# Attention's output products taken two tiles at a time, a rotary table repeated through DRAM, and a parity mask spread by loads

## The chip, the cores and the metric

The kernel runs on one core of one Trainium2 chip. Its time is in microseconds (us) of the device for one whole execution, from launch to the last store. All engines of the core run beside each other, each through its own list of instructions in order: PE (matrix products), ACT (copies and functions), DVE (elementwise work), POOL (elementwise work and masks), and SP (it only issues DMA transfers). An instruction begins when everything it waits for on other engines has been signalled. Products accumulate in PSUM banks; everything else stands in SBUF, 128 partitions wide.

## What the kernel computes

One decoder block over 1024 positions and 1024 channels: a norm, one wide input projection, two mixers that work from it, a merge, and a gated convolutional MLP. The parts that the change touches are those of the attention mixer:

```python
proj = h @ w_in[layer]
z_a, q, k, v, gate_logits = jnp.split(proj, splits, axis=-1)
q = apply_partial_rope(q.reshape(b, s, N_ATTN_HEADS, HEAD_DIM), cos, sin)
k = apply_partial_rope(k.reshape(b, s, N_ATTN_HEADS, HEAD_DIM), cos, sin)
# three groups of 4 heads: (window, dilation) = (128,1), (512,4), (2048,16)
for g, (window, dil) in enumerate(DILATED_GROUPS):
    o, lse = banded_window_attention(residue(q), residue(k), residue(v), window // dil)
alpha = softmax(lses over the groups)
y_b = einsum('bshg,bshgd->bshd', alpha, o_all)          # groups mixed by their denominators
```

Rotary turning covers the first quarter of each head's 64 channels (`t1*cos - t2*sin`, `t1*sin + t2*cos`). In group 1 a position's residue is its number modulo 4; in group 2 modulo 16, where the kernel puts two residues into one tile of 128 positions and a parity mask keeps them apart.

## The kernel before

**Products.** The large matrix products are taken in float32 as three products of split parts. Each weight block is split into a high part (`hi`, an ACT copy, L313) and a remainder (`lo`, a DVE subtraction, L314). The input projection goes by pairs of column blocks, numbered n (from 3 or 4 on in what follows; 5 and 6 are the ones looked at). For each pair PE makes seven products in the order P1, P6, P2, P7, P5, P4, P3, each 12 matmuls of 128x512 (L545). Their split weights stand in a ring of four slots in `G1` (`OPS_IN = 4`): the split for one product can be written only when the product four places earlier is done. Before P6 of a pair come three DVE sums of weight blocks (L278, L279, L280); L278 makes the block that P7 uses (`wt`, one buffer), L280 the one that P6 uses. Before P4 comes L283.

**Results.** P1 is copied out of its bank by ACT (L573); P2 then accumulates into the same bank as P1, after that copy; P2 is copied out by ACT (L577). P6, P7, P5, P4 and P3 are added to the copied values by DVE (L575, L580, L582, L585, L588). There are three such banks. P7's bank is the one that P4 uses two products later, and P5's is the one that P3 uses.

**Side work.** Everything that isn't an input product is hung between them by due times: `after(lag, fn)` runs `fn` so many half products (6 matmuls) later. Pairs 0 to 2 are the gating mixer's, then come three pairs of each attention group (q and k with their rotary part, the rest of q and k, v), groups in the order 1, 2, 0, and then the rest. In each group eight tiles T of 128 queries follow each other, every five half products: load, turn (scale), scores (`sc`), transposes of the probabilities (`pp`), and the product with v (`pu`, L935, 8 or 16 small matmuls), whose result ACT copies with stride 4 (group 1) or 8 (group 2) into a tile `o` of the whole group (L942), or without a stride into `YC` (group 0). After the last tile `o` is stored to DRAM.

**Rotary table.** Angles and sines are made by DVE, POOL and ACT in [position, (block, frequency)] form, spread over heads by 16 ACT copies, transposed by 4 x 4 PE transposes (`rot`, L2537), and copied into `YC` by ACT (L2538). `rope` (L794 to L796) applies it: six DVE operations for a pair, whose operand from `YC` is read with stride 4 in group 1, 8 in group 2 and 1 in group 0, and then four stores (L798).

**Parity mask.** One small matmul of a sign vector by itself (`pg`, L1099), a DVE operation, a POOL selection.

**Mix.** After the three groups, `mix_groups` loads for each half of the positions, each channel half and each group the weights `wb` and (groups 1 and 2) the outputs `ob`, multiplies them on DVE (L1057) and adds them to `YC` (L1060).

**Order.** PE's order is as written throughout. ACT's and DVE's are as written until product 18 of the input projection; behind it, and for SP's DMA issues everywhere, the framework's scheduler sets them when the kernel is built.

Of the kernel before, what the change touches and what calls it, by code (L numbers as in the profile page):

```python
# [20 lines left out]
P = 128  # L21
# [73 lines left out]
def block_kernel(  # L95
# [711 lines left out]
    def by_channel(t):  # L807
        return t.rearrange("(c p) s -> p c s", p=P)
# [7 lines left out]
    class Attend:  # L816
# [5 lines left out]

        def __init__(self, g, T, vts, out):
            self.g, self.T, self.vts, self.out = g, T, vts, out
# [86 lines left out]
        def turn_p(self):  # L911
            pT = at.tile([P, NH * 2, P], F32, name=f"pT_{self.name}", tag="pT", bufs=1)
# [14 lines left out]
        def product(self):  # L927
            pu = ps_x.tile([P, 2, P], F32, name=f"pu_{self.name}", tag="pu")
            n = len(self.parts)
            for pair in range(2):  # L930
                for k, s in enumerate(self.parts):
                    vt = self.vts[self.halves[s]]
                    for h in (2 * pair, 2 * pair + 1):
                        r = h % 2 * HD
                        nc.tensor.matmul(  # L935
                            pu[r : r + HD, pair, :],
                            vt[:, h * HD : (h + 1) * HD],
                            self.pT[:, h * n + k, :],
                            start=k == 0,
                            stop=k == n - 1,  # L940
                        )
# [4 lines left out]
        def columns(self):  # L946

            T = self.T
            if self.g == 0:
                return self.out[:, :, T * P : (T + 1) * P]  # L950
            if self.g == 1:
                r, bb = T // 2, T % 2
                return self.out[:, :, bb * HALF + r : (bb + 1) * HALF : 4]
            return self.out[:, :, T::8]

        def start(self, s):
            after(max(1, s - 4), self.load)
            after(s, self.turn)
            after(s + 3, self.score)
            after(s + 8, self.turn_p)  # L960
            after(s + 13, self.product)

    def attention(g, ct):
# [14 lines left out]
        out = at.tile([P, 2, S], F32, name=f"o_{g}", tag="o", bufs=1) if g else YC  # L978
        for T in range(8):
            Attend(g, T, vts, out).start(4 + 5 * T)  # L980
# [54 lines left out]
    def mix_groups(pool):  # L1035
# [5 lines left out]
        def load(h, c, g):  # L1041
# [8 lines left out]
            if g:  # L1050
                o = pool.tile([P, HALF], F32, name=f"ob_{h}_{c}_{g}", tag="ob", bufs=4)
                nc.sync.dma_start(o, by_channel(summed_d[g])[:, c, hs])
            got[h, c, g] = wb, o

        def mix(h, c, g):
            wb, o = got[h, c, g]
            tt(o, o, wb, ALU.mult)  # L1057
            if g:
                y = YC[:, c, h * HALF : (h + 1) * HALF]
# [12 lines left out]
    def open_attention():  # L1072
# [8 lines left out]
        sign = at.tile([P, 2, 256], F32, name="sign", tag="vt", bufs=4)[0:1, 0, 0:P]  # L1081
        nc.gpsimd.memset(mask, 0.0)
        nc.gpsimd.memset(sign[:, 0::2], 1.0)
        nc.gpsimd.memset(sign[:, 1::2], -1.0)
# [19 lines left out]
        after(8, parity_mask)  # L1104

# [77 lines left out]
    rot_halves = []  # L1183

    def rot_bank(name):
        if not rot_halves:
            t = ps_x.tile([P, 2, HALF], F32, name=name, tag="sc")
            rot_halves.extend((t[:, 1], t[:, 0]))
        return rot_halves.pop()
# [1405 lines left out]
```

## Time and profile before

| | us |
|---|---|
| median of 3 runs | 1343.32 (1343.31 to 1344.57) |
| the profiled execution, whole | 1342.83 |
| its span, first to last instruction | 1341.0 |
| what lies around the span | 1.83 |
| PE busy in the span | 1332.4 (99%) |
| DVE busy | 1037.5 (77%) |
| ACT busy | 648.4 (48%) |
| POOL busy | 283.9 (21%) |

The granted TensorE clock was 0.999 on the mean. The busy share of an engine says how much of the span it had an instruction running; only the engine on the chain that ended last sets the time directly. A matmul's record is some 0.39 us long for 128x512, but the next one begins 0.227 us after it (12 matmuls in 2.72 us), so stretches on PE are read from one start to the next.

### The profile page before, as it was taken

What the parts mean: (1) busy time and instruction counts of PE and PEld (TensorE: products, weight loads), DVE (VectorE), ACT (ScalarE), POOL (GpSimd) and SP (SyncE); (2) the same over time, 40 slices, a digit from 0 to 9 for tenths busy, and PEclk for the clock granted to TensorE, in tenths of its full rate; (3) what the DMA queues carried; (4) which work ended last, traced back from release to release, by engine and by line L of the source; (5) the groups of instructions that cost most, each with busy time, mean ns of one, the idle gap of its engine ahead of it and who ended that gap; (6) DMA issues with size and microseconds to landing.
All of it is one profiled execution on the core that took longest, in us unless ns stands there. A gap on an engine that the chain in (4) does not pass through costs nothing.

```text
span 1341.0 us, 19015 instructions
## 1 busy us (share of the span) xinstructions
PE 1332.4 (99%) x6405; PEld 1100.5 (82%) x6405; DVE 1037.5 (77%) x1808; ACT 648.4 (48%) x1267; POOL 283.9 (21%) x270
## 2 busy tenths in 40 slices
PE   9999999999999999999999999999999999999997
PEld 8888888888888888888888888888888888888886
DVE  7989696886768957759789789777777778576675
ACT  7762566666633325245365333433343335454453
POOL 1121000000000000120010337656565653000002
PEclk9999999999999999999999999999999999999999
DMA  9436444545439733975650324444445538986663
GB/s 353 108 98 186 118 139 132 159 148 168 130 107 273 272 108 121 300 254 189 198 178 17 126 97 154 166 165 165 163 151 173 175 123 293 396 313 222 197 205 126
DMA packets 148305, 240.19 MB, mean 179 GB/s; under 512 B 18320, under 2 KB 58864, under 8 KB 148208
## 3 DMA queue, kind: packets, MB, share of 16 engines
q1 hardware_dynamic: 145968, 234.99, 53.6%
q0 software_dynamic: 1088, 2.10, 0.9%
q10 hardware_dynamic: 1152, 1.89, 0.4%
q8 instruction: 51, 0.84, 0.3%
q14 instruction: 46, 0.38, 0.1%
HBM read 170.91 MB, written 64.34 MB: 175 GB/s over the span
## 4 chain that ended last, share of the span: by engine, by line
PE 98%; DVE 1%; ACT 0%; issue 0%; POOL 0%; POOLq 0%; DVEq 0%; ACTq 0%
PE in_P L545 30%; PE uP L2016 21%; PE dn L2298 15%; PE up L2016 9%; PE wo_P L1847 5%; PE pa L1477 5%; PE pl L618 3%; PE pu L1996 2%; PE pb L1477 2%; PE pu L935 1%; PE pp L916 1%; PE pm L733 1%; PE sc L865 1%; PE ht L1751 1%; PE sc L869 0%; PE avt L971 0%
## 5 line engine op out<-in xcount | busy, mean ns | idle before, releaser
L545 PE MATMUL in_P<-R,G 128*128 128x512 f32 x1008 | 237.3, 391 | 0.0
L545 PEld LDWEIGHTS in_P<-R,G 128*128 128x128 f32 x1008 | 187.4, 188 | 38.8 <-issue 0.3
L2298 PE MATMUL dn<-R 128*128 128x512 f32 x924 | 209.6, 389 | 0.0
L2298 PEld LDWEIGHTS dn<-R 128*128 128x128 f32 x924 | 173.4, 188 | 36.0
L170 ACT ACTIVATE R<-up 128x512 fp32r<-128x512 f32 x109 | 65.8, 623 | 122.9 <-DVE up L280 105.6
L2016 PE MATMUL uP<-G,R 128*128 128x512 f32 x504 | 121.4, 389 | 0.0
L2016 PE MATMUL uP<-R 128*128 128x512 f32 x504 | 121.1, 389 | 0.0
L313 ACT ACTIVATE G<-wr 128x512 fp32r<-128x512 f32 x126 | 78.4, 628 | 88.1 <-PE in_P L545 61.2
L2016 PE MATMUL up<-G,R 128*128 128x512 f32 x504 | 120.3, 389 | 0.0
L545 PE MATMUL in_P<-G,G 128*128 128x512 f32 x504 | 119.9, 391 | 0.0
L314 DVE TENSOR_TENSOR G<-wr,G 128x512 fp32r<-128x512 f32 x126 | 86.7, 689 | 42.7 <-ACT G L313 41.8
L2016 PEld LDWEIGHTS uP<-G,R 128*128 128x128 f32 x504 | 94.4, 188 | 20.2 <-issue 0.4
L2016 PEld LDWEIGHTS up<-G,R 128*128 128x128 f32 x504 | 94.6, 188 | 19.7
L2016 PEld LDWEIGHTS uP<-R 128*128 128x128 f32 x504 | 94.6, 188 | 19.6
L545 PEld LDWEIGHTS in_P<-G,G 128*128 128x128 f32 x504 | 93.7, 188 | 19.6 <-issue 0.3
L171 POOL TENSOR_TENSOR G<-wbs,G 128x512 fp32r<-128x512 f32 x12 | 17.0, 1432 | 437.9 <-ACT G L170 437.9
L171 POOL TENSOR_TENSOR R<-up,R 128x512 fp32r<-128x512 f32 x55 | 79.4, 1456 | 13.4 <-ACT R L170 12.1
L170 ACT ACTIVATE R<-db 128x512 fp32r<-128x512 f32 x77 | 48.0, 625 | 53.4 <-PE dn L2298 43.8
L171 DVE TENSOR_TENSOR R<-db,R 128x512 fp32r<-128x512 f32 x77 | 53.6, 700 | 24.9 <-ACT R L170 24.8
L1477 PE MATMUL pa<-R,G 128*128 128x512 f32 x288 | 67.9, 389 | 0.0
L1477 PEld LDWEIGHTS pa<-R,G 128*128 128x128 f32 x288 | 54.1, 188 | 11.2
L545 PE MATMUL in_P<-G 128*128 128x512 f32 x252 | 61.5, 391 | 0.0
(303 smaller groups left out, 2355.3 us busy)
## 6 DMA issues: line engine op xcount, KB each, us to landing
up<-in_w_up_dram SPq DMA_DIRECT2D x44, 512.0 KB, 4.1
wr<-in_w_in_dram SPq DMA_DIRECT2D x42, 512.0 KB, 4.1
dA<-gd SPq DMA_DIRECT2D x55, 256.0 KB, 4.7
dS<-gS SPq DMA_DIRECT2D x44, 256.0 KB, 4.5
db<-wT SPq DMA_DIRECT2D x44, 256.0 KB, 4.5
gd<-Y SPq DMA_DIRECT2D x42, 256.0 KB, 2.0
db<-in_w_down_dram SPq DMA_DIRECT2D x33, 256.0 KB, 4.9
gated<-C SPq DMA_DIRECT2D x32, 256.0 KB, 2.4
```

Of the source, the lines that this page charges most:

```text
L170: nc.scalar.activation(hi, src, AF.Copy)
L171: fn = lambda: lo_eng.tensor_tensor(lo, src, f32(hi), ALU.subtract)
L313: lambda: nc.scalar.activation(op[:, 0], src, AF.Copy),
L314: lambda: nc.vector.tensor_tensor(op[:, 1], src, f32(op[:, 0]), ALU.subtract),
L545: nc.tensor.matmul(acc, op[:, w, kt, :], left[LEFT[name], kt][:, a, :], start=opened and i == 0, stop=i == len(HIGH_FIRST) - 1, skip_group ...
L618: nc.tensor.matmul(lead_banks[b][:, cs], raw_x[h, kt][:, a, c * P : (c + 1) * P], lead_op(kt, w, cs), start=kt == 0 and p == 0 and cs.star ...
L733: nc.tensor.matmul(acc[hs], v[:, hs], wspT[:, (c * 2 + s) // 3, :], start=True, stop=True)
L1477: nc.tensor.matmul(acc, unit[a][kt // 4][:, kt % 4, :], two(R, 8 * h + kt)[:, b, :], start=n == 0 and i == 0, stop=n == len(kts) - 1 and i ...
L1847: nc.tensor.matmul(acc, left[LEFT[name], kt][:, a, blk * P : (blk + 1) * P], out_ops[s][:, w, :], start=name not in SHARED and kt == 0 and ...
L1996: nc.tensor.matmul(acc, plain_up[which, k][:, w, kt, :], left[f"A{h + 1}{k + 1}", kt][:, a, :], start=n == 0 and i == 0, stop=n == KT - 1 ...
L2016: nc.tensor.matmul(acc, op[w][:, kt, :], left[LEFT[name], kt][:, a, :], start=opened and i == 0, stop=i == len(HIGH_FIRST) - 1, skip_group ...
L2298: nc.tensor.matmul(accs[blk], dops[s][:, 0, a, blk * P : (blk + 1) * P], dops[s][:, 1, w, :], start=SEQ[j] not in CONTINUES and kt == 0 an ...
```

## The change

Four edits in one diff.

1. *Two tiles per output product.* An even tile T only keeps its transposed probabilities (two buffers of `pT`); the odd tile makes the products of both into one bank and copies 128x512 at once. In groups 1 and 2 the copy is contiguous, into a small tile `o` that is stored to DRAM for each pair of tiles.
2. *Mix.* `ob` is therefore loaded in residue order, and `wb` and the piece of `YC` are read (and `YC` written) through views with stride 4 (group 1) or 8 (group 2). In group 2 `ob` comes by two loads.
3. *Rotary table.* One PE transpose of the sines, two ACT copies, three stores to DRAM, eight DMAs inside DRAM that repeat the rows over heads, and one load into `YC`.
4. *Parity mask.* POOL writes two rows with alternating entries; they go to DRAM and come back by two loads, each spread over 64 partitions. `causal` follows at a due time of its own.

```diff
-    summed_d = {g: dram.tile([256, S], F32, name=f"od{g}") for g in (1, 2)}
+    summed_d = {g: dram.tile([4, P, 2, 2, P], F32, name=f"od{g}") for g in (1, 2)}
+    stripe_d = dram.tile([1, 2, P], F32, name="stripe")
...
-            pT = at.tile([P, NH * 2, P], F32, name=f"pT_{self.name}", tag="pT", bufs=1)
+            pT = at.tile([P, NH * 2, P], F32, name=f"pT_{self.name}", tag="pT", bufs=2)
...
         def product(self):
-            pu = ps_x.tile([P, 2, P], F32, name=f"pu_{self.name}", tag="pu")
...
-            nc.scalar.activation(self.columns(), pu, AF.Copy)
-            if self.T == NB - 1 and self.g:
-                nc.sync.dma_start(by_channel(summed_d[self.g]), self.out)
+            pu = ps_x.tile([P, 2, 2, P], F32, name=f"pu_{self.name}", tag="pu")
+            for t, one in enumerate((self.before, self)):
+                n = len(one.parts)
+                for pair in range(2):
+                    for k, s in enumerate(one.parts):
+                        vt = one.vts[one.halves[s]]
+                        for h in (2 * pair, 2 * pair + 1):
+                            r = h % 2 * HD
+                            nc.tensor.matmul(
+                                pu[r : r + HD, t, pair, :],
...
+            T0 = self.T - 1
+            if self.g == 0:
+                dst = YC[:, :, T0 * P : (T0 + 2) * P].rearrange("p c (t q) -> p t c q", t=2)
+                nc.scalar.activation(dst, pu, AF.Copy)
+            else:
+                o = at.tile([P, 2, 2, P], F32, name=f"o_{self.name}", tag="o", bufs=2)
+                nc.scalar.activation(o, pu, AF.Copy)
+                nc.sync.dma_start(summed_d[self.g][T0 // 2], o)
...
-            after(s + 13, self.product)
+            if self.before:
+                after(s + 13, self.product)
...
-                nc.sync.dma_start(o, by_channel(summed_d[g])[:, c, hs])
-            got[h, c, g] = wb, o
+                src = summed_d[g]
+                if g == 1:
+                    nc.sync.dma_start(
+                        o.rearrange("p (r q) -> p r q", r=4), src[:, :, h, c, :].rearrange("r p q -> p r q")
+                    )
+                else:
+                    js = slice(h * HD, (h + 1) * HD)
+                    for t in range(2):
+                        nc.sync.dma_start(
+                            o.rearrange("p (r t q) -> p t r q", r=4, t=2)[:, t],
+                            src[:, :, t, c, js].rearrange("r p q -> p r q"),
+                        )
+
+            y = YC[:, c, hs]
+            if g:
+                r = 4 * g
+                o = o.rearrange("p (r j) -> p r j", r=r)
+                wb, y = (ap.rearrange("p (j r) -> p r j", r=r) for ap in (wb, y))
+            got[h, c, g] = wb, o, y
...
         def parity_mask():
-            pg = tr_tile("pg")
-            nc.tensor.matmul(pg[:, :P], sign, sign, start=True, stop=True)
-            nc.vector.tensor_scalar(mask2, pg[:, :P], 1.0, -0.5 * NEG, ALU.subtract, ALU.mult)
-            causal(mask2)
+            for r in range(2):
+                nc.sync.dma_start(
+                    mask2[r::2], stripe_d[:, r].partition_broadcast(64).rearrange("q o t -> q (o t)")
+                )
...
-            for fn in wide[:4]:
-                fn()
...
-        elif i in (15, 16, 17, 18):
+        elif i in (13, 14, 15):
             turns.pop(0)()
...
-    def turn(i, c):
-        pt = bank(f"rot_{i}_{c}")
-        for k in range(4):
-            ks = slice(k * P, (k + 1) * P)
-            nc.tensor.transpose(pt[:, ks], wides[i][c][:, ks], ident)
-        nc.scalar.activation(out[:, i, c * HALF : (c + 1) * HALF], pt, AF.Copy)
+    def turn():
+        pt = bank("rot")
+        nc.tensor.transpose(pt[:, 0:P], lent[:, W : 3 * W], ident)
+        flat, neg = lent[:, 4 * W : 6 * W], lent[0:W, 6 * W : 8 * W]
+        nc.scalar.activation(flat, pt[:, 0:P], AF.Copy)
+        nc.scalar.activation(neg, pt[0:W, 0:P], AF.Copy, scale=-1.0)
+        nc.sync.dma_start(table[1], flat[0:W])
+        nc.sync.dma_start(table[0], flat[W:])
+        nc.sync.dma_start(table[2], neg)
+
+    def repeat():
+        full = wide.rearrange("i (r f h) s -> i r f h s", r=4, f=NF)
+        for i, k, r0, r1 in ((0, 0, 0, 4), (1, 2, 0, 2), (1, 1, 2, 4)):
+            src = table[k].rearrange("(f b) q -> f (b q)", f=NF).unsqueeze(1)
+            for r in range(r0, r1):
+                nc.sync.dma_start(full[i, r], src.to_broadcast([NF, NH, S]))
+
+    def load():
+        nc.sync.dma_start(out, wide.rearrange("i p s -> p i s"))
```

The lists that the build makes of the two kernels differ as follows at three places. A row is the line, the operation, what it writes and what it reads; the numbers behind names tell buffers apart.

ACT around the first two products of pair 5, before (`C_103<-in_P_1333` are the copies of P1, L573, and of P2, L577; `wr_0_910` and `wr_1_969` are the weights of pair 5, and `G_76` is the ring):

```order
100 L313 ACTIVATE G_76<-wt_5_1184 128x512
101 L573 ACTIVATE C_103<-in_P_1333 128x4x128
102 L313 ACTIVATE G_76<-wr_1_969 128x512
103 L313 ACTIVATE G_76<-wr_0_910 128x512
104 L577 ACTIVATE C_103<-in_P_1333 128x4x128
```

The same place in the changed kernel (pair 5's `wr_0` is `wr_0_909` there, its P1 bank `in_P_1314`):

```order
94 L313 ACTIVATE G_76<-wt_5_1170 128x512
95 L313 ACTIVATE G_76<-wr_1_969 128x512
96 L313 ACTIVATE G_76<-wr_0_909 128x512
97 L573 ACTIVATE C_103<-in_P_1314 128x4x128
98 L577 ACTIVATE C_103<-in_P_1314 128x4x128
```

The copy of P1 moved from ahead of the high parts for P5 (`wr_1`) and P4 (`wr_0`) to behind both.

DVE around the weight sums of pair 6, before (`wr_1_1329` and `wr_0_1288` are pair 6's weights, `wt_6` the block for its P7; the L575 to L588 rows add the products of pair 5):

```order
167 L278 TENSOR_TENSOR wt_6_1433<-wr_1_1329 128x512
168 L575 TENSOR_TENSOR C_103<-C_103,in_P_1349 128x4x128
169 L314 TENSOR_TENSOR G_76<-wr_0_910,G_76 128x512
170 L279 TENSOR_TENSOR wr_1_1329<-wr_1_1329,wr_0_1288 128x512
171 L314 TENSOR_TENSOR G_76<-wr_1_969,G_76 128x512
172 L580 TENSOR_TENSOR C_103<-C_103,in_P_1403 128x4x128
173 L314 TENSOR_TENSOR G_76<-wr_0_1288,G_76 128x512
174 L280 TENSOR_TENSOR wr_0_1288<-wr_1_1329 128x512
175 L582 TENSOR_TENSOR C_103<-C_103,in_P_1419 128x4x128
176 L314 TENSOR_TENSOR G_76<-wr_0_1288,G_76 128x512
177 L585 TENSOR_TENSOR C_103<-C_103,in_P_1403 128x4x128
```

And in the changed kernel, where six `rope` operations stand right behind L575 of pair 5 (pair 6's weights are `wr_1_1310` and `wr_0_1269`):

```order
174 L582 TENSOR_TENSOR C_103<-C_103,in_P_1402 128x4x128
175 L585 TENSOR_TENSOR C_103<-C_103,in_P_1386 128x4x128
176 L314 TENSOR_TENSOR G_76<-wr_0_1269,G_76 128x512
177 L588 TENSOR_TENSOR C_103<-C_103,in_P_1402 128x4x128
178 L278 TENSOR_TENSOR wt_6_1416<-wr_1_1310 128x512
179 L279 TENSOR_TENSOR wr_1_1310<-wr_1_1310,wr_0_1269 128x512
180 L314 TENSOR_TENSOR G_76<-wt_6_1416,G_76 128x512
181 L280 TENSOR_TENSOR wr_0_1269<-wr_1_1310 128x512
182 L314 TENSOR_TENSOR G_76<-wr_1_1310,G_76 128x512
183 L283 TENSOR_TENSOR wr_0_1269<-wr_0_1269 128x512
184 L314 TENSOR_TENSOR G_76<-wr_0_1269,G_76 128x512
```

The three sums moved behind L588, the last addition of pair 5, and the remainder of P7's weights (row 180) now stands between L279 and L280; the last row is the remainder for P6. On ACT the same place of the changed kernel reads (rows of pair 6):

```order
100 L313 ACTIVATE G_76<-wr_0_1269 128x512 x2
101 L573 ACTIVATE C_104<-in_P_1458 128x8x64
102 L313 ACTIVATE G_76<-wt_6_1416 128x512
103 L313 ACTIVATE G_76<-wr_1_1310 128x512
104 L313 ACTIVATE G_76<-wr_0_1269 128x512
```

The copy of P1 of pair 6 (L573) stands ahead of the high parts for P7, P5 and, last of the three, P6; before, those for P6, P2 and P7 all stood ahead of that copy.

DVE in the mix, before (`ob_0_1` and `ob_0_2` are the outputs of groups 1 and 2; L580 and L582 take P7 and P5 of a pair out of their banks):

```order
687 L1057 TENSOR_TENSOR ob_0_1_4234<-ob_0_1_4234,wb_0_1_4231 128x512
688 L1060 TENSOR_TENSOR YC<-YC,ob_0_1_4234 128x512
689 L674 TENSOR_TENSOR ya<-ya,C_103 128x512
690 L314 TENSOR_TENSOR G_76<-wr_1_3996,G_76 128x512
691 L1057 TENSOR_TENSOR ob_0_2_4281<-ob_0_2_4281,wb_0_2_4278 128x512
692 L1060 TENSOR_TENSOR YC<-YC,ob_0_2_4281 128x512
693 L580 TENSOR_TENSOR C_103<-C_103,in_P_4200 128x512
```

The same place in the changed kernel:

```order
687 L1072 TENSOR_TENSOR ob_0_1_4206<-ob_0_1_4206,wb_0_1_4203 128x512
688 L1074 TENSOR_TENSOR YC<-YC,ob_0_1_4206 128x4x128
689 L674 TENSOR_TENSOR ya<-ya,C_103 128x512
690 L314 TENSOR_TENSOR G_76<-wr_1_3967,G_76 128x512
691 L580 TENSOR_TENSOR C_103<-C_103,in_P_4172 128x512
692 L314 TENSOR_TENSOR G_76<-wr_0_4086,G_76 128x512
693 L1072 TENSOR_TENSOR ob_0_2_4253<-ob_0_2_4253,wb_0_2_4250 128x512
694 L280 TENSOR_TENSOR wr_0_4086<-wr_1_4107 128x512
695 L1074 TENSOR_TENSOR YC<-YC,ob_0_2_4253 128x8x64
696 L582 TENSOR_TENSOR C_103<-C_103,in_P_4190 128x512
```

The multiplication and addition of group 2 moved from ahead of L580 to between L580 and L582, and the additions are through views of 4x128 and 8x64.

## Rows read from the trace of the kernel before

**Rows 1.** The page, busy time (share, instructions) and the chain that ended last.

```profile
PE 1332.4 (99%) x6405; PEld 1100.5 (82%) x6405; DVE 1037.5 (77%) x1808; ACT 648.4 (48%) x1267; POOL 283.9 (21%) x270
...
PE 98%; DVE 1%; ACT 0%; issue 0%; POOL 0%; POOLq 0%; DVEq 0%; ACTq 0%
```

**Rows 2.** Waits of PE: engine, line, waited for: us in total, times, longest.

```profile
PE warm L396 <- POOL ident masks.py:199: 1.7, 1, 1.7
```

**Rows 3.** Timeline of PE around output products: start us, us, engine, line, operation.

```profile
173.10 0.66 PE L935 MATMUL pu<-pT,v 128*64 128x128 f32 x8
173.69 1.09 PE L916 MATMUL pp<-ident,pr 128*128 128x128 f32 x8
...
341.18 1.52 PE L545 MATMUL in_P<-G 128*128 128x512 f32 x6
342.63 1.09 PE L935 MATMUL pu<-pT,v 128*64 128x128 f32 x16
343.65 1.09 PE L916 MATMUL pp<-ident,pr 128*128 128x128 f32 x8
```

**Rows 4.** Timeline of PE at the table's transposes and at the sign product.

```profile
102.56 0.66 PE L2537 MATMUL rot<-ident,YC 128*128 128x128 f32 x4
102.97 0.71 PE L545 MATMUL in_P<-R,G 128*128 128x512 f32 x2
...
142.84 0.48 PE L1099 MATMUL pg<-sign 1*128 1x128 f32 x2
143.26 0.97 PE L545 MATMUL in_P<-G 128*128 128x512 f32 x3
```

**Rows 5.** Timeline of ACT, first products of pair 5; brackets: idle before, and releaser.

```profile
129.35 0.60 ACT L573 ACTIVATE C<-in_P 128x512 f32<-128x512 f32 x1 [3.82 <-PE in_P L545]
129.85 0.62 ACT L313 ACTIVATE G<-wr 128x512 fp32r<-128x512 f32 x1
132.12 0.63 ACT L313 ACTIVATE G<-wr 128x512 fp32r<-128x512 f32 x1 [1.65 <-PE in_P L545]
```

**Rows 6.** Timelines of ACT and of DVE around pair 6.

```profile
149.05 0.60 ACT L573 ACTIVATE C<-in_P 128x512 f32<-128x512 f32 x1 [2.03 <-PE in_P L545]
149.54 0.62 ACT L313 ACTIVATE G<-wr 128x512 fp32r<-128x512 f32 x1
...
132.31 0.68 DVE L575 TENSOR_TENSOR C<-C,in_P 128x512 f32<-128x512 f32 x1
...
138.22 0.69 DVE L314 TENSOR_TENSOR G<-wr,G 128x512 fp32r<-128x512 f32 x1
138.95 0.69 DVE L280 TENSOR_TENSOR wr<-wr 128x512 f32<-128x512 f32 x1
...
146.41 0.68 DVE L588 TENSOR_TENSOR C<-C,in_P 128x512 f32<-128x512 f32 x1
```

**Rows 7.** Timeline of SP, a store behind rope; page, issues: KB each, us to landing.

```profile
126.25 0.34 SPq L798 DMA_DIRECT2D qd<-C  x1
...
wr<-in_w_in_dram SPq DMA_DIRECT2D x42, 512.0 KB, 4.1
```

**Rows 8.** Two tiles: duration ns min/median/max, first and last start us, forms.

```profile
L794 DVE TENSOR_TENSOR swap<-swap,YC x6: 683/1066/1189, 123.0 to 251.9; 128x512 f32<-128x512 f32 x6
...
L942 ACT ACTIVATE o<-pu x16: 617/662/688, 173.8 to 311.9; 128x256 f32<-128x256 f32 x16
```

**Rows 9.** Window 412 to 450 (PE PEld DVE ACT POOL, PEclk, DMA); timelines of DVE, PE.

```profile
412.00:450.00 38.00, 38.00 (x170) 31.45 (x169) 36.62 (x60) 14.11 (x24) 0.00 (x0) 1.00 0.89 266
...
427.64 0.68 DVE L1057 TENSOR_TENSOR ob<-ob,wb 128x512 f32<-128x512 f32 x1
...
428.97 0.68 DVE L580 TENSOR_TENSOR C<-C,in_P 128x512 f32<-128x512 f32 x1
...
430.89 0.68 DVE L582 TENSOR_TENSOR C<-C,in_P 128x512 f32<-128x512 f32 x1
...
427.49 5.60 PE L545 MATMUL in_P<-G,G 128*128 128x512 f32 x24
```

More of the change, by code (lines that the diff above doesn't have):

```diff
@@ L816, in block_kernel, with __init__ @@
     class Attend:
-        def __init__(self, g, T, vts, out):
-            self.g, self.T, self.vts, self.out = g, T, vts, out
+        def __init__(self, g, T, vts, before):
+            self.g, self.T, self.vts, self.before = g, T, vts, before
             self.has_prev = (g == 0 and T > 0) or (g == 1 and T % 2 == 1)
@@ L927, in product @@
         def product(self):
-            pu = ps_x.tile([P, 2, P], F32, name=f"pu_{self.name}", tag="pu")
[L929 to L941, printed above, removed]
@@ new lines, in product @@
+            for t, one in enumerate((self.before, self)):
[7 more added lines that the diff above has]
+                                pu[r : r + HD, t, pair, :],
+                                vt[:, h * HD : (h + 1) * HD],
+                                one.pT[:, h * n + k, :],
+                                start=k == 0,
+                                stop=k == n - 1,
+                            )
@@ L977, in attention @@
             after(lag, lambda T=T: turn_v(T), first=True)
-        out = at.tile([P, 2, S], F32, name=f"o_{g}", tag="o", bufs=1) if g else YC
+        before = None
         for T in range(8):
-            Attend(g, T, vts, out).start(4 + 5 * T)
+            one = Attend(g, T, vts, before)
+            one.start(4 + 5 * T)
+            before = None if before else one
         if not g:
@@ L1181, in block_kernel @@
     ps_x_stack = ExitStack()
[L1183 to L1189, printed above, removed]
+    rope_d = dram.tile([3, NB * ROT // 2, P], F32, name="rope")
+    rope_w = dram.tile([2, P, S], F32, name="rope_w")
     def beginning():
         nc.scalar.dma_start(chan, per_channel)
-        chain, wide, turns = rot_tables(
-            nc, lent, [[YC[:, i, lower], YC[:, i, upper]] for i in range(2)],
-            rot_bank, ident, pos, YC,
-        )
+        chain, turns = rot_tables(nc, lent, tr_tile, ident, pos, rope_d, rope_w, YC)
         def some(n):
@@ L1300, in beginning @@
             x_sum_dma(4, k)
-        return some, lambda: len(chain), wide, turns, a22, s3
+        return some, lambda: len(chain), turns, a22, s3
     late = {}
@@ L1382, in block_kernel @@
     )
-    some, steps_left, wide, turns, a22, s3 = beginning()
+    some, steps_left, turns, a22, s3 = beginning()
     WD_START = in_order.index((NP_IN - 3, "P6"))
@@ L2456, in finish_rms, with rot_tables @@
     return rs
-def rot_tables(nc, lent, wides, bank, ident, pos, out):
+def rot_tables(nc, lent, bank, ident, pos, table, wide, out):
     NF = ROT // 2
@@ L2517, in rot_tables @@
     steps.append(sines)
-    def widen(i, c, rep):
-        nc.scalar.activation(
-            wides[i][c].rearrange("p (b r f h) -> p r b f h", b=4, r=4, h=NH)[:, rep],
-            (cs, sn)[i][:, 4 * c * NF : 4 * (c + 1) * NF].rearrange("p (b f) -> p b f", b=4)
-            .unsqueeze(3).to_broadcast([P, 4, NF, NH]),
-            AF.Copy,
-            scale=-1.0 if i == 1 and rep < 2 else 1.0,
-        )
-    for i in range(2):
-        for c in range(2):
-            for rep in range(4):
-                spreads.append(lambda i=i, c=c, rep=rep: widen(i, c, rep))
-    def turn(i, c):
-        pt = bank(f"rot_{i}_{c}")
-        for k in range(4):
-            ks = slice(k * P, (k + 1) * P)
-            nc.tensor.transpose(pt[:, ks], wides[i][c][:, ks], ident)
-        nc.scalar.activation(out[:, i, c * HALF : (c + 1) * HALF], pt, AF.Copy)
-    turns = [lambda i=i, c=c: turn(i, c) for i in range(2) for c in range(2)]
-    return steps, spreads, turns
+    def turn():
[15 more added lines that the diff above has]
+        nc.sync.dma_start(out, wide.rearrange("i p s -> p i s"))
+    turns = [turn, repeat, load]
+    return steps, turns
 def tiled(w, cols):
```

32 lines of the change are left out of this document (10 added, 22 removed).

## The prediction

> **What bounds the kernel now.** I read the chain of work that ended last first: 98% of it is PE, with DVE busy 77% and ACT 48% beside it [rows 1]. Then the waits of PE: one, 1.7 us, at the very start [rows 2]. So PE runs without a gap from its first product to the last. Two things follow. An instruction that leaves PE is saved in full. And nothing that leaves DVE, ACT or SP is worth anything by itself; any piece of their work that comes later than PE needs it is paid in full. So I looked for what PE drops, and then, in the order of instructions after the change, for each place at which an operand or a bank comes later than before, and took the durations from the timelines.
>
> **What leaves PE.** An output product of 16 small matmuls takes 343.65 - 342.63 = 1.02 us up to the transposes behind it, one of 8 takes 173.69 - 173.10 = 0.59 [rows 3]. Eight more matmuls are thus 0.43, and 1.02 - 2 x 0.43 = 0.16 is paid once per run, however many there are. Ahead of it six input matmuls take 342.63 - 341.18 = 1.45 instead of 1.36 (half of 2.72), 0.09 more. There are 24 such runs and will be 12, and the matmuls stay: 12 x (0.16 + 0.09) = 3.0 us. A set of four table transposes takes 102.97 - 102.56 = 0.41 [rows 4]; four sets are 1.64, one transpose (a quarter of a set, 0.1) stays: 1.54 us. The sign product takes 143.26 - 142.84 = 0.42 [rows 4]. Sum: 5.0 us less, all on the path.
>
> **First new wait: P2 of pair 5.** P2 accumulates where ACT must first have copied P1. Before, that copy begins at 129.35, as soon as P1 is done [rows 5]. In the changed order two high parts stand ahead of it on ACT, and the second, for P4, takes the slot of P6 and so waits for P6's end: this is the copy that starts at 132.12 after idling for PE [rows 5]. On ACT the next instruction begins 0.50 after such a one (129.85 - 129.35), so the copy of P1 would run from 132.62 to 133.22, and P2 start 0.04 later. PE would have begun P2 at about 131.92: the last of P6's records ends near 132.08, each is 0.39 long and the next begins 0.227 after it. Cost 1.3 us. Bounds: at least the copy alone, 0.6, should the high part for P4 get its slot early; no more than the 1.3, in which nothing lies beside anything.
>
> **Second new wait: P6 of pair 6.** Before, L280 (the block for P6) runs at 138.95 and the product comes some 10 us later [rows 6]. In the changed order the three sums stand behind L588 of pair 5, which waits for the end of P3, and L280 behind the remainder of P7's weights, whose high part ACT makes after the copy of P1 of pair 6. That copy starts at 149.05 [rows 6]. From there: the high part for P7 at 149.54 for 0.62, its remainder on DVE at 150.20, L280 0.73 later (138.95 - 138.22) for 0.69, to 151.62, and the high part for P6 to 152.28. PE wanted P6 at 148.85 (0.16 before the copy could begin, as above). 152.32 - 148.85 = 3.5 us. All that stands behind on DVE and ACT moves with it, and PE has nothing else in its list to do meanwhile. Bounds: 3.0 if ACT finds its part a little earlier, and upward 1:1 with the load of these weights. In the changed list of SP that load stands behind the four stores of `rope` and two more. `rope` follows L575, at about 132.9 [rows 6]; four operations of 1.07 and two of 0.68 [rows 8] end at 138.5, six stores of some 0.4 (0.34 at the first, [rows 7]) at 140.9, and the load lands 4.1 later [rows 7], at 145.0. L278 can't begin before 146.41 + 0.6 [rows 6], so 2 us of cover are left; a landing at 8 us, twice the usual, would add 2.
>
> **The mix.** DVE is busy 36.62 of the 38 us from 412 to 450 [rows 9]; it has no room there, only a lead over PE. The tightest points: L580 empties P7's bank, and P4 takes it. P5 and P4 are the 24 matmuls that begin at 427.49, so P4 begins at 430.21; L580 ends at 428.97 + 0.68 = 429.65: 0.56 of lead. L582 ends at 430.89 + 0.68 = 431.57, P3 begins at 432.93: 1.36 of lead. The added strides first: a contiguous operation takes 0.683, the rotary one with one operand at stride 4 1.066 and at stride 8 up to 1.189 [rows 8], that is 0.38 more, and up to 0.51, of which I take 0.45. Each multiplication has one such operand. Each addition has two, a read and a write, which no row of DVE shows. If reading and writing run beside each other, an addition costs what a multiplication does; if they add up, 0.76 and 0.90. ACT's copies with a strided write take 0.662 for 256 elements, more than a contiguous 512 (0.60) [rows 5, 8], so writes do cost. I take 0.5 and 0.6. Up to L580 of pair 17 there are multiplications and additions of groups 1, 2 and 1: 1.21 + 1.6 = 2.8 more, less the group 2 pair that stands behind L580 now (428.97 - 427.64 = 1.33): 1.48, less the lead of 0.56: 0.9 us. Up to L582 that pair is back, with 1.05 more: 3.86 - 0.9 - 1.36 = 1.6. Together 2.5 us. With strides that cost nothing 0; with one side 2.0 by the same sums; with both sides added 3.6.
>
> [...]
>
> **What is hidden.** The table's way through DRAM is three transfers one after another, begun no later than the first set of transposes stood (102.56, [rows 4]) and needed at 132.9; even at 8 us each it is in time. ACT loses 16 spreading copies and half of the output copies and is on no chain. The parity mask is used in group 2 alone, long after its loads. The transposes that leave let PE reach DVE's work between pairs earlier than DVE gains (two rotary operations of 1.07 move out of that stretch); this can give back part of the 1.54, never more: 0 to 1.5, I take 0.8, half. A late `ob` (two loads with short rows in group 2) adds to the mix 1:1; none counted.
>
> **Sum.** -5.0 + 1.3 + 3.5 + 2.5 + 0.8 = +3.1 us. On the profiled execution, 1342.83 (span 1341.0 and 1.83 around it), 1345.9; the median of the runs is 0.49 above that execution, so 1346.4.
>
> **Rivals.** *The mix costs nothing.* The lead of DVE, or strides that run beside each other, cover it, and the 0.8 too: -5.0 + 4.8 = -0.2, 1343.1; with one of both, up to 1345. For it: DVE is idle for 23% of the span [rows 1], so its lead may be larger elsewhere than at the two points. Against: the strided rows and the small leads. This is the side of no change. *Strided additions pay both sides and `ob` lands late*: +1.1, and 1 to 2 us of waiting for a load (a quarter to a half of the usual 4.1 more), +5.2 to 6.2: 1348.5 to 1349.5; the same figure comes if the weights of pair 6 land at 8 us. For it: SP issues more between the same loads, and the DMA share is 0.89 in that stretch [rows 9]. *The two waits at pairs 5 and 6 don't come*, because the split parts are ready by another way than I read from the lists: -5.0, with the mix -2 at most: 1338.3 to 1341. Against it: these orders are fixed when the kernel is built. It decides by whether the high part for P4 really has to wait for P6.
>
> **Chances.** My sum 0.47 (its own range 1345.0 to 1348.0), no cost in the mix 0.22, the dearer mix or a late load 0.2, no waits 0.11. A difference under 0.2% (2.7 us, 1340.6 to 1346.0) can't be told from none here. Of the last case 0.1 is faster; of my sum a third lies below 1346.0, which with the second case and the rest makes 0.40; slower is 0.50. Leaving out a tenth at either side: 1340.8 to 1350.0.
>
> **What would show it.** Right: PE with a wait of about 1.3 before P2 near 130 and of about 3.5 before P6 near 150, for ACT both; `pu` in 12 runs; the additions at L1074 at 1.0 to 1.3 us, and waits for DVE near 430. Wrong: no PE wait near 150 (the order on DVE and ACT then let P6's parts through), additions at 0.69, or a wait at scores or `rope` for the table.

## The result and the profile after

The changed kernel takes 1348.28 us (median of 9 runs, 1346.7 to 1349.32), against 1343.32 for the kernel before: 4.96 us more, ratio 1.0034 with a 95% interval of 1.0026 to 1.0043. The forecast was 1346.4 in a range of 1340.8 to 1350.0; the direction was right and the loss 1.9 us larger than forecast.

The page of the changed kernel, its span, busy times and the chain that ended last (to be laid beside [rows 1]):

```profile
span 1346.5 us, 18970 instructions
...
PE 1328.6 (99%) x6388; PEld 1099.2 (82%) x6388; DVE 1042.8 (77%) x1807; ACT 638.6 (47%) x1237; POOL 281.8 (21%) x271
...
PE 86%; DVE 7%; DMA 2%; ACT 2%; issue 1%; SPq 1%; DVEq 0%; POOLq 0%; ACTq 0%; POOL 0%
```

PE has 17 instructions fewer and is busy 3.8 us less, yet the span is 5.5 us longer, and the chain that was 98% PE is 86% PE now. The 14% of that chain off PE are not the loss: behind a wait the chain follows the late engine back for as long as that engine was never idle, mostly before 126 us and from 400 to 438. The loss is in PE's own waits, which this list names (engine, line and what it waited for: us in total, times, longest; [rows 2] had one line):

```profile
PE in_P L545 <- ACT G L313: 3.2, 1, 3.2
PE warm L396 <- POOL ident masks.py:199: 1.7, 1, 1.7
PE rot L2522 <- DVE V L738: 1.5, 1, 1.5
PE in_P L545 <- ACT C L573: 1.3, 1, 1.3
PE in_P L545 <- DVE C L582: 1.0, 1, 1.0
PE in_P L545 <- DVE C L580: 0.7, 1, 0.7
PE uP L2017 <- DVE Y L2038: 0.6, 1, 0.6
PE in_P L545 <- DVE st L899: 0.6, 1, 0.6
PE pp L914 <- ACT v L969: 0.3, 1, 0.3
```

Behind the familiar start wait stand eight new ones, 9.2 us together. The largest stands where the forecast put it, before P6 of pair 6. PE's timeline there, then two windows (busy PE, PEld, DVE, ACT, POOL, granted clock, DMA share, GB/s):

```profile
152.73 5.70 PE L545 MATMUL in_P<-R,G 128*128 128x512 f32 x18 [3.19 <-ACT G L313]
```

```profile
152.20:155.50 3.30, 2.77 (x7) 2.20 (x8) 3.23 (x6) 1.74 (x3) 0.57 (x1) 0.50 0.78 237
155.60:158.20 2.60, 2.60 (x13) 2.13 (x12) 1.46 (x3) 0.63 (x1) 0.00 (x0) 1.00 0.20 58
```

Besides the wait of 3.19 us there is a second price that the forecast didn't have. The 18 matmuls behind it should take 18 x 0.227 = 4.1 us and a last record's 0.16, and their block is 5.70 long: the granted clock was at 0.50 of full when the wait ended, with matmuls beginning 0.43 us apart, and back at 1.00 from 155.60. From the wait at pair 5 to this one PE had run without a gap; in it PE did nothing. That block lost some 1.5 us.

The chain that makes the wait, on ACT and DVE (to be laid beside [rows 6]):

```profile
149.57 0.60 ACT L573 ACTIVATE C<-in_P 128x512 f32<-128x512 f32 x1 [4.81 <-PE in_P L545]
150.07 0.62 ACT L313 ACTIVATE G<-wt 128x512 fp32r<-128x512 f32 x1
...
152.05 0.63 ACT L313 ACTIVATE G<-wr 128x512 fp32r<-128x512 f32 x1 [0.84 <-DVE wr L280]
```

```profile
146.85 0.69 DVE L588 TENSOR_TENSOR C<-C,in_P 128x512 f32<-128x512 f32 x1 [1.36 <-PE in_P L545]
147.46 0.69 DVE L278 TENSOR_TENSOR wt<-wr 128x512 f32<-128x512 f32 x1
...
150.72 0.69 DVE L314 TENSOR_TENSOR G<-wt,G 128x512 fp32r<-128x512 f32 x1 [1.85 <-ACT G L313]
151.33 0.68 DVE L280 TENSOR_TENSOR wr<-wr 128x512 f32<-128x512 f32 x1
```

Step by step it is the forecast: the copy of P1 at 149.57, the high part for P7 at 150.07, its remainder on DVE at 150.72 after 1.85 us of idling for it, L280 at 151.33, the high part for P6 at 152.05, and PE at 152.73. L278 began 0.61 after L588 without idling, so the weights of pair 6 had landed by then.

At P2 of pair 5, PE and ACT (beside [rows 5]):

```profile
125.89 5.78 PE L545 MATMUL in_P<-R,G 128*128 128x512 f32 x24
132.93 5.73 PE L545 MATMUL in_P<-R,G 128*128 128x512 f32 x24 [1.25 <-ACT C L573]
```

```profile
131.76 0.63 ACT L313 ACTIVATE G<-wr 128x512 fp32r<-128x512 f32 x1 [2.09 <-PE in_P L545]
132.29 0.58 ACT L573 ACTIVATE C<-in_P 128x512 f32<-128x512 f32 x1
```

The second high part idles for the end of P6, and the copy L573 follows it: 1.25 us of waiting on PE, forecast 1.3. The profile counts a wait from the end of the last record, which is 0.16 after the next matmul could have begun. From start to start this one cost 132.93 - (125.89 + 5.78 - 0.16) = 1.42, and the longer one 3.35.

The third large wait was not forecast at that size. PE where the four sets of transposes used to begin:

```profile
94.42 0.30 PE L2522 MATMUL rot<-ident,ones 128*128 128x128 f32 x1 [1.51 <-DVE V L738]
```

The one transpose waits 1.51 us for a DVE addition (L738). It writes one of the two banks that the spatial products (`pm`) rotate through, and DVE, which empties those, is behind there.

In the mix, PE and the two kinds of operation (duration ns min/median/max):

```profile
434.07 2.99 PE L545 MATMUL in_P<-G,G 128*128 128x512 f32 x12 [0.67 <-DVE C L580]
438.03 2.32 PE L545 MATMUL in_P<-G 128*128 128x512 f32 x9 [0.97 <-DVE C L582]
```

```profile
L1072 DVE TENSOR_TENSOR ob<-ob,wb x8: 1057/1105/1217, 403.6 to 447.9; 128x512 f32<-128x512 f32 x8
```

```profile
L1074 DVE TENSOR_TENSOR YC<-YC,ob x8: 1052/1132/1220, 404.7 to 450.1; 128x512 f32<-128x512 f32 x8
```

The waits stand at L580 and L582, as forecast, 0.67 and 0.97. An addition with two strided sides takes 1.13, a multiplication with one 1.10: the strided result adds nothing to speak of to the strided operand, which was the lower of the two cases.

The gain on PE is there too. Two merged runs (beside [rows 3]):

```profile
334.82 1.52 PE L545 MATMUL in_P<-R,G 128*128 128x512 f32 x6
336.27 1.53 PE L935 MATMUL pu<-pT,v 128*64 128x128 f32 x24
337.73 1.09 PE L914 MATMUL pp<-ident,pr 128*128 128x128 f32 x8
338.58 1.20 PE L863 MATMUL sc<-kring,qs 128*128 128x256 f32 x8
```

```profile
355.19 1.97 PE L935 MATMUL pu<-pT,v 128*64 128x128 f32 x32
357.09 1.09 PE L914 MATMUL pp<-ident,pr 128*128 128x128 f32 x8
```

And transposes (`pp`) ahead of which the run of an even tile has gone:

```profile
346.45 1.03 PE L914 MATMUL pp<-ident,pr 128*128 128x128 f32 x8
347.24 0.96 PE L863 MATMUL sc<-kring,qs 128*128 128x256 f32 x6
```

24 matmuls take 1.46 us, where 16 and 8 took 1.02 + 0.59; 32 take 1.90, where twice 16 took 2.04. To these 0.14 to 0.15 come the 0.09 ahead of a run and 0.06 behind it, which the forecast didn't have: eight transposes take 0.85 up to the next product behind a run and 0.79 where there is none. That is 0.29 to 0.30 for each of 12 runs, 3.6 us and not the 3.0 forecast. The starts of the same matmuls in the two traces, laid side by side, give 3.6 as well.

### The profile page after: what moved, and what is told of

Same layout as the page of the kernel before. It is cut to its first block, busy times and chain, and to the rows that moved or that the text cites. A ratio compares the mean times of both kernels' runs of the same rounds, so it can differ in the third digit from the quotient of the medians.

```text
span 1346.5 us, 18970 instructions
## 1 busy us (share of the span) xinstructions
PE 1328.6 (99%) x6388; PEld 1099.2 (82%) x6388; DVE 1042.8 (77%) x1807; ACT 638.6 (47%) x1237; POOL 281.8 (21%) x271
## 4 chain that ended last, share of the span: by engine, by line
PE 86%; DVE 7%; DMA 2%; ACT 2%; issue 1%; SPq 1%; DVEq 0%; POOLq 0%; ACTq 0%; POOL 0%
PE in_P L545 24%; PE uP L2017 20%; PE dn L2299 15%; PE up L2017 8%; PE wo_P L1848 5%; PE pa L1478 5%; PE pu L1997 2%; PE pb L1478 2%; PE pp L914 1%; PE pu L935 1%; DMA wb<-share 1%; DVE X L488 1%; PE sc L863 1%; PE pm L733 1%; DVE G L314 1%
## 5 line engine op out<-in xcount | busy, mean ns | idle before, releaser
L2017 PE MATMUL uP<-G,R 128*128 128x512 f32 x504 | 121.4, 390 | 0.6 <-DVE Y L2038 0.6
L2017 PE MATMUL uP<-R 128*128 128x512 f32 x504 | 121.1, 389 | 0.0
L2017 PE MATMUL up<-G,R 128*128 128x512 f32 x504 | 120.2, 389 | 0.0
L314 DVE TENSOR_TENSOR G<-wr,G 128x512 fp32r<-128x512 f32 x126 | 86.8, 689 | 42.3 <-ACT G L313 41.4
L2017 PEld LDWEIGHTS uP<-G,R 128*128 128x128 f32 x504 | 94.5, 188 | 20.8 <-issue 1.0
L2017 PEld LDWEIGHTS up<-G,R 128*128 128x128 f32 x504 | 94.6, 188 | 19.6
L2017 PEld LDWEIGHTS uP<-R 128*128 128x128 f32 x504 | 94.6, 188 | 19.6
```

Of the source, the lines that this page charges most:

```text
L314: lambda: nc.vector.tensor_tensor(op[:, 1], src, f32(op[:, 0]), ALU.subtract),
L2017: nc.tensor.matmul(acc, op[w][:, kt, :], left[LEFT[name], kt][:, a, :], start=opened and i == 0, stop=i == len(HIGH_FIRST) - 1, skip_group ...
```

## The experiments

Ratios are those of the runs against the kernel before on the same chip, with a 95% interval. "The changed kernel" is the starting point unless another is named.

**Order kept as written.** What it tells apart: whether the waits at pairs 5 and 6 are the loss, or something later.

```diff
-        if i == ORDERED:
+        if i == 30:
             ordered.close()
```

> The changed kernel, with the written order of ACT and DVE kept until product 24 of the input projection instead of 18, so that the copy of P1 of pair 5 stands ahead of the high parts and the weight sums of pair 6 ahead of L582. Theory (the two waits, with the slower clock behind the longer one, are paid in full): the waits of 1.3 us before P2 of pair 5 and 3.2 us before P6 of pair 6 go, and 1.4 us of slow matmuls behind the second: 1348.3 - 5.9 = 1342.4 us, no PE wait over 0.5 us between 125 and 160 us, clock 1.00 there. Rival A (the clock has nothing to do with that wait): 4.5 us less, 1343.8, and slow matmuls still near 150. Rival B (the time is lost in the mix, and what is won at 130 to 150 us is waited for again later): not below 1347.

The kernel that ran kept the order until product 30, as the diff shows, and not 24; the later ones have 24. Measured: 1341.16 us, ratio 0.9985 (0.9977 to 0.9994). The two longest waits of PE behind the start:

```profile
PE rot L2522 <- DVE V L738: 1.5, 1, 1.5
PE in_P L545 <- DVE C L582: 1.0, 1, 1.0
```

Both waits are gone, and the granted clock over the whole run is 0.999 (0.998 in the changed kernel). From 1348.28 to 1341.16 is 7.1 us. The two waits, from start to start, and the slow matmuls are 1.42 + 3.35 + 1.5 = 6.3 of it. Small waits that are shorter here make up the rest as far as these two profiles show: 0.2 at L899, 0.4 at L580 and 0.3 at `uP` (near 760 us). Rival B falls, and rival A with it: no matmuls near 150 us are slow in this profile. The changed kernel with this edit is faster than before by 0.15%.

**The table's transpose in its old bank.**

```diff
-        chain, turns = rot_tables(nc, lent, tr_tile, ident, pos, rope_d, rope_w, YC)
+        chain, turns = rot_tables(
+            nc, lent,
+            lambda name: ps_x.tile([P, 2, HALF], F32, name=name, tag="sc")[:, 0],
+            ident, pos, rope_d, rope_w, YC)
```

> The changed kernel, with the one table transpose written to the bank that the four sets used before, not to the two banks shared with the spatial products. Theory: its wait of 1.5 us near 93 us was for a bank that DVE had not emptied, and goes: 1346.8 us. Rival A (it waited for the sines, which ACT's function table load delays): the wait stays within 0.3 us of 1.5, 1348.3. Rival B (PE gets to the next DVE-bound place earlier and waits there): 1347.5 to 1348.3, with other waits between 95 and 125 us.

Measured: 1346.9 us, ratio 1.0027 (1.0018 to 1.0036). PE at the same place:

```profile
93.30 0.33 PE L2524 MATMUL rot<-ident,ones 128*128 128x128 f32 x1
```

No wait any more: it was the bank, not the sines. The gain of 1.4 is near the 1.5 expected, though the intervals of the two kernels overlap; rival B falls by the trace, which has no new wait from 95 to 125 us. This kernel still has the wait of 3.19 us before P6, and behind it the block and the slow window read:

```profile
151.60 6.98 PE L545 MATMUL in_P<-R,G 128*128 128x512 f32 x18 [3.19 <-ACT G L313]
```

```profile
150.40:157.10 6.70, 5.50 (x13) 4.34 (x14) 4.37 (x7) 1.89 (x3) 0.34 (x1) 0.50 0.56 161
```

The same wait, but the same 18 matmuls take 6.98 us instead of 5.70: some 12 intervals of 0.43 us instead of 0.227. So the price behind a wait is not fixed: 1.5 us in one run, 2.7 in another. How much of the next stretch runs at 0.50 differs from run to run while the wait is the same to 0.01 us. The profile of the third experiment, which leaves this place as it is, has a third case:

```profile
153.11 6.30 PE L545 MATMUL in_P<-R,G 128*128 128x512 f32 x18 [3.19 <-ACT G L313]
```

```profile
153.15:154.75 1.60, 1.56 (x6) 0.99 (x7) 1.60 (x3) 0.80 (x2) 0.00 (x0) 1.00 0.91 195
154.80:158.10 3.30, 3.30 (x10) 2.55 (x9) 1.76 (x4) 0.70 (x2) 0.00 (x0) 0.50 0.31 117
```

Here the clock fell only some 1.6 us after PE had taken up work again, and 2.1 us were lost.

**The multiplications of the mix on POOL.**

```diff
-            tt(o, o, wb, ALU.mult)
+            (nc.gpsimd.tensor_tensor if g else tt)(o, o, wb, ALU.mult)
```

> The changed kernel, with the multiplications of groups 1 and 2 in the mix on POOL, which is idle there, instead of DVE (8 operations of 1.1 us less on DVE from 400 to 450 us). Theory (DVE's added strided time makes the waits at L580 and L582 near 434 and 438 us): both waits go, 2.1 us less, 1346.2 us. Rival A (the loads of ob with short rows are what comes late): the waits stay, 1348.3. Rival B (POOL is slower than DVE, 1.4 us or more for such an operation, and the additions behind it come late or hold DVE up): 1348 to 1350.

Measured: 1350.75 us, ratio 1.0056 (1.0043 to 1.0068), slower than the changed kernel. Groups of POOL and DVE from 395 to 480 us (busy us, mean ns, idle before and its releaser):

```profile
L1072 POOL TENSOR_TENSOR ob<-ob,wb 128x512 f32<-128x512 f32 x8 | 14.9, 1863 | 282.1 <-DMA ob<-od 282.1
```

```profile
L1074 DVE TENSOR_TENSOR YC<-YC,ob 128x512 f32<-128x512 f32 x8 | 9.0, 1131 | 3.7 <-POOL ob L1072 3.7
L279 DVE TENSOR_TENSOR wr<-wr,wr 128x512 f32<-128x512 f32 x4 | 5.5, 1383 | 0.0
```

A multiplication takes 1.86 us on POOL, and DVE idles 3.7 us ahead of the additions for them, in the same list in which the emptying of banks stands. Nor was DVE relieved as expected. Six of its contiguous operations with two operands in SBUF that run beside a multiplication on POOL (at L278, L279, L314 and L674) take 1.46 to 2.12 us in place of 0.69, 7.4 us more in all, against the 8.9 us of multiplications that left DVE; the mean at L279 doubles. The waits of PE at L575 and L580 come to 3.7 us there, 2.1 more than the two in the changed kernel. Rival B; it says nothing on the strides, so that question went to the sixth experiment.

**The parity mask undone.**

```diff
+            pg = tr_tile("pg")
+            nc.tensor.matmul(pg[:, :P], sign, sign, start=True, stop=True)
+            nc.vector.tensor_scalar(mask2, pg[:, :P], 1.0, -0.5 * NEG, ALU.subtract, ALU.mult)
+            causal(mask2)
...
-            for r in range(2):
-                nc.sync.dma_start(
-                    mask2[r::2], stripe_d[:, r].partition_broadcast(64).rearrange("q o t -> q (o t)")
-                )
...
-        after(14, lambda: causal(mask2))
```

> The changed kernel, with the parity mask made by the small matmul as before (the other three edits stay). In the order of instructions this alone brings the weight sums of pair 6 back ahead of L588 and P6's high part ahead of the copy of P1; the copy of P1 of pair 5 stays behind the two high parts. Theory: the 3.2 us wait before P6 of pair 6 and the 1.4 us of slow matmuls go, the sign product costs 0.4 again: 1348.3 - 4.6 + 0.4 = 1344.1 us, with the wait of 1.3 us near 131 us still there. Rival A (the slow matmuls are not tied to the wait): 1345.5. Rival B (rope and its stores hold the weights of pair 6 back whatever the mask does): the wait stays, 1348.7.

Measured: 1346.79 us, ratio 1.0022 (1.0013 to 1.0031): between theory and rival B, and neither. PE's timeline says why:

```profile
151.48 3.06 PE L545 MATMUL in_P<-R,G 128*128 128x512 f32 x12 [0.28 <-ACT G L313]
156.01 1.66 PE L545 MATMUL in_P<-R,G 128*128 128x512 f32 x6 [1.48 <-ACT C L573]
```

The wait before P6 of pair 6 shrank to 0.28, but the high parts that moved ahead now hold up the copy of P1, and P2 of pair 6 waits 1.48 for it, as P2 of pair 5 still waits 1.25. The expectation had left that out. The granted clock is 1.00 from 137 to 140 and from 150 to 160 us, and the 24 matmuls behind the wait of 1.25 take 5.73 us, as in the changed kernel, whose clock is 1.00 from 131.50 to 140: behind waits of 1.25 and 1.48 no matmul is slow.

**Order and bank together.** The edits of the first two (with 24).

> The changed kernel with both mends: written order of ACT and DVE until product 24, and the table's transpose in its old bank. Theory (the waits stand at different places and add up): 1341.2 (order alone) - 1.5 (bank alone) = 1339.7 us. Rival (a DVE-bound stretch between 95 and 130 us gives the bank's gain back once the order is as written): 1340.8 to 1341.2.

Measured: 1339.67 us, ratio 0.9972 (0.9961 to 0.9983). The two gains add up, as far as the intervals of the times tell.

**The same, with the mix's weights in residue order.**

```diff
-        nc.tensor.transpose(pt[0:n, 0:P], share["w"], ident)
+        for g in range(3):
+            nc.tensor.matmul(
+                pt[g * k : (g + 1) * k, 0:P], share["w"][:, g * k : (g + 1) * k],
+                ident.rearrange("p (j r) -> p r j", r=4 * g or 1), start=True, stop=True,
+            )
...
-                wb, y = (ap.rearrange("p (j r) -> p r j", r=r) for ap in (wb, y))
+                wb = wb.rearrange("p (t r j) -> p r t j", t=4, r=r)
+                y = y.rearrange("p (j r) -> p r j", r=r)
```

> The same with the weights of the mix turned into residue order by the matmul that transposes them (three products with a permuted identity instead of one transpose, 0.2 to 0.4 us more on PE), so that the multiplications of groups 1 and 2 read wb in runs of 32 or 16 elements; the additions keep their stride. Theory (the strided operands on DVE make the waits near 430 us): these multiplications fall from 1.1 to 0.7 us, 3.4 us less on DVE, the waits of some 1.3 us at L580 and L582 go or fall under 0.3: 1338.7 us. Rival A (late loads of ob, not the strides): multiplications at 0.7 us, the waits stay, 1340. Rival B (runs of 16 cost as much as single elements): multiplications stay at 1.1 us.

Measured: 1338.99 us, ratio 0.9967 (0.9956 to 0.9979). The multiplications from 390 to 470 us, and all waits of PE behind the start:

```profile
L1080 DVE TENSOR_TENSOR ob<-ob,wb 128x512 f32<-128x512 f32 x8 | 5.5, 685 | 0.0
```

```profile
PE in_P L545 <- DVE st L899: 1.1, 1, 1.1
PE uP L2029 <- DVE Y L2050: 0.5, 1, 0.5
PE pp L914 <- ACT v L969: 0.3, 1, 0.3
```

The multiplications are back at 0.685 in runs of 32 or 16 elements, the additions (L1084) stay at 1.136 on the mean, and both waits of the mix are gone, where the fifth experiment's profile has 0.9 and 0.7. The loads are the same in both, so this speaks for the strides on DVE and against late loads. It is one profile: the two waits together are 0.3 to 1.6 us in the eight other profiles with this strided mix on DVE, and missing in none of them. The times of the fifth and sixth kernels (1339.67 and 1338.99) don't separate by their intervals; the sixth is the fastest kernel of the study, faster than both given ones.

**Edits 1 and 2 alone.** The table and the mask as in the kernel before (their parts of the diff undone).

> The kernel before with edits 1 and 2 alone (products of two tiles in one run, and the mix with strides); table and parity mask as before. Theory: 3.0 us less on PE, 1.7 to 2.1 us of waits in the mix, 0.4 at a score: 1343.3 - 3.0 + 2.3 = 1342.6 us, no wait at pairs 5 and 6. Rival A (this edit alone already shifts the order behind product 18): waits near 130 or 150 us, 1347. Rival B (the saving per run is smaller than 0.25 us): 1344 to 1345.

Measured: 1341.46 us, ratio 0.9987 (0.9979 to 0.9996). The largest new wait on PE is 0.9 us (L582, in the mix); none at pairs 5 and 6. The two-tile products pay off even with the strided mix: 1.9 us of the 3.6 remain.

**The control for the order.** The same edit, with 24, in the kernel before.

> The kernel before with the written order kept until product 24 and nothing else: the control for the order. Theory (before had no wait on PE to remove): 1343.3 us, within 0.7. Rival (the written order is better by itself, and what it won in the changed kernel is not that kernel's waits): 1341 or less.

Measured: 1343.45 us, ratio 1.0002 (0.9994 to 1.0011). The written order by itself is worth nothing there. What it won in the first experiment was the changed kernel's own waits.

**One long wait.** The first experiment's edit with 20 in place of 30, which moves `rope` ahead of L585.

> The changed kernel with the written order kept until product 20: the six rope operations then stand on DVE ahead of L585 of pair 4, which must empty the bank that P6 of pair 5 uses; so one wait of some 6 to 7.5 us near 125 us, and neither of the waits at pair 5's P2 and pair 6's P6. Theory (a wait of PE also costs the slow clock behind it, 1.6 to 2.9 us behind the waits of 3.2 us so far): 1341.2 + 7 + 2 = 1350.2 us, with matmuls 0.43 us apart behind the wait. Rival A (the clock answers only to the wait's length, so twice the wait costs twice the slow time): 1352.5. Rival B (the slow matmuls belong to that place near 150 us, for instance to the transfers there, not to the wait): 1348.2, no slow matmuls behind this wait.

Measured: 1351.55 us, ratio 1.0066 (1.0048 to 1.0084), between the theory and rival A and a little nearer to rival A, so the trace has to decide. PE, and the window from 137 to 140 us:

```profile
136.65 10.29 PE L545 MATMUL in_P<-R,G 128*128 128x512 f32 x36 [7.53 <-DVE C L585]
```

```profile
137.00:140.00 3.00, 3.00 (x8) 2.32 (x8) 3.00 (x10) 0.00 (x0) 0.00 (x0) 0.50 0.70 187
```

The wait is 7.53 us, at another place and for another reason, and behind it the clock is at 0.50 and the 36 matmuls take 10.29 us instead of 36 x 0.227 + 0.16 = 8.33: 2.0 us lost. From 148 to 160 us the clock is 1.00. So the slow stretch belongs to the wait and not to the place (rival B falls), and more than twice the wait did not cost twice the slow time (rival A falls, for this one profiled run). The clock had fallen to 0.50 some 2.9 us before this wait ended, so that part of it met no work.

**The rotary table undone.** Edits 1, 2 and 4 stay.

> The changed kernel with the rotary table as before (edits 1, 2 and the mask stay). Theory (the table's way through DRAM is what shifts the order behind product 18; the mask's loads alone do not): no wait at pairs 5 and 6, 1341.5 (edits 1 and 2 alone) - 0.4 for the sign product = 1341.1 us. Rival (the mask's loads hold the weights of pair 6 back too): a wait of 3 us near 150, 1345.

Measured: 1340.88 us, ratio 0.9985 (0.9975 to 0.9994); on PE 1.0 and 0.2 us in the mix and 0.3 at `pp`, nothing at pairs 5 and 6. So the edit of the table (its transposes, its loads and their due times, which were not told apart) is what the waits there need; without it the mask's loads cost nothing. With it, the fourth experiment shows, the edit of the mask decides which product of pair 6 waits: P6 for 3.19, or P2 for 1.48.

## Why the forecast came out as it did

- *PE runs without a gap, so what it drops is saved and what it waits for is paid.* Right, and the first experiment and the control show it: the waits removed came back as time, in the kernel that had them and only there.
- *5.0 us leave PE.* The output runs gave 3.6 instead of 3.0, because a run also costs 0.06 behind it. The 1.54 of the transposes are right as a length, but 1.51 of it was taken back at the very transpose that stayed. The sign product's 0.42 is consistent with the last experiment beside the seventh (1340.88 and 1341.46, whose intervals overlap), not more.
- *P2 of pair 5, 1.3.* Measured 1.25 (1.42 from start to start, as the forecast counted), by the chain as forecast.
- *P6 of pair 6, 3.5.* The wait is 3.19 (3.35 from start to start), by the chain as forecast. What is missing is the clock: the sum counted the wait alone, as if PE went on at full clock behind it. The slow matmuls add 1.5 in the profiled run, 2.7 and 2.1 in those of the second and third experiments.
- *The mix, 2.5.* Measured 1.64 (0.67 and 0.97), and 0.3 to 1.6 in the other profiles with these strides on DVE. I had taken a strided addition at 0.5 to 0.6 us more than a contiguous one, between the two cases; it is 0.44 more (1.13 against 0.69), what a multiplication pays. Strides on both sides of these additions were paid once. By the forecast's own sums that gives 2.0; the rest was not followed up. The multiplications took 1.10 with one strided operand against 0.69, and were back at 0.685 with runs of 32 or 16 elements in the sixth experiment.
- *What is hidden, 0.8.* The table was in time, as forecast: no wait at `rope`. But that the transposes which leave let PE reach DVE's work earlier, so that part of the gain comes back, was the wrong mechanism. What made PE wait was a bank that the edit changed from `ps_x` to the ring of `pm`, which the sum didn't price: there the transpose waited 1.51 us for that ring's reader (L738), and in its old bank, in the second experiment, not at all. With 0.6 at L899 and 0.3 at `pp` the new small waits are 2.4 instead of 0.8, and this term is as far off as the clock. The 0.6 at `uP` L2017 (near 768 us) is 0.3 to 0.5 or absent in other profiles, so it isn't put down to the change.
- *The account.* 5.6 us left PE (3.6, 1.54 and 0.42); 9.2 of waits as listed, some 1 us more of them from start to start, and 1.5 of slow matmuls came. That is some 6.1, against the 5.5 by which the spans of the two profiled executions differ and the 4.96 between the medians. Something that is no effect of the change lies between: the first input product begins at 48.34 in the profiled execution of the changed kernel and at 49.43 in that of the kernel before, in code that is the same in both. The trace's first record of the granted clock at 1.00 begins 5.4 us behind the span's start in one and 7.9 in the other; matmuls begin 0.21 us apart ahead of it and 0.12 behind it, and from 5.45 to 7.80 PE ran 21 of them in one and 13 in the other. Over all profiles that product begins between 48.0 and 49.4. With this 1.1 the account comes to some 5.0, and 0.5 of the 5.5 stays unexplained.
- *Luck.* The time is 0.3 above the 1345.0 to 1348.0 that the forecast gave its own sum. That it came so near is in part luck: the clock (+1.5) and the small waits (+1.6) were too low, the mix (2.5 for 1.6) too high and the saving on PE (5.0 for 5.6) too small, and these misses partly cancel.
- *Rivals.* "The mix costs nothing" and "the two waits don't come" fell. "Strided additions pay both sides" gave a time near the measured one (1348.5), and for the wrong reason: additions pay once, and no `ob` came late.

What stays open: how long the clock stays low behind a given wait. The same 3.19 us gave 1.5, 2.1 and 2.7 us of loss in three profiles. The clock fell inside the wait in two of them and behind it in the third, and came back at different times; what decides was not tried.

## What to carry to other kernels

On an engine that never waits, a change is worth its saved instructions minus every operand that now comes late, so compare the built order of the engines that feed it, and not the diff alone: here an edit of DMAs and of one table moved a copy on ACT behind two others and a weight sum on DVE behind five additions, in code that the diff doesn't touch. A result that accumulates into a bank another engine must first copy, and a tile moved into another pool's banks, are the places to look at first (1.25 and 1.51 us here). And price more than the length of a wait of several us on TensorE: here 3.19 us cost 1.5 to 2.7 us of slow matmuls on top.

## What the runs showed of the hardware that was not expected

- At or shortly behind the end of a wait of 3.19 us (three profiles) and of 7.53 us (one) the granted clock is at 0.50, and 128x512 matmuls begin 0.43 us apart instead of 0.227, for 6 to 12 matmuls; behind waits of 1.25 and 1.48 us none does.
- A float32 addition on DVE with one operand and the result at stride 4 or 8 takes 1.05 to 1.22 us, the same as a multiplication with one strided operand and a contiguous result (1.06 to 1.22). With that operand in runs of 32 or 16 elements the multiplication takes 0.685, as a contiguous one does.
- Such a multiplication on POOL took 1.86 us on the mean (1.52 to 2.71), though POOL had nothing else to do, and DVE operations with two operands in SBUF that ran beside it took up to 2.12 us in place of 0.69.
